# Other widths for the two parts of the last down projection, an earlier norm of the first, and work moved from GpSimd to VectorE

## The chip, the core and the metric

The kernel runs on one core of a Trainium2 chip. Its metric is the device time in microseconds of one launch; lower is better. The kernel computes a whole decoder layer, and the change concerns its last 35 microseconds.

## The reference

One layer of a hybrid decoder for a prompt of 512 tokens and 8 sample sequences of 4 tokens, 544 tokens in all, with 1024 features. Dilated attention, a gated recurrence and a cross attention come first; they are not touched. What matters here is the end, which both groups of tokens share:

```python
def rmsnorm(x, g):
    x32 = x.astype(jnp.float32)
    y = x32 * lax.rsqrt(jnp.mean(x32 * x32, axis=-1, keepdims=True) + EPS)
    return (y * g.astype(jnp.float32)).astype(x.dtype)
...
    x = x + (jax.nn.silu(conv) * (u @ w_up)) @ w_down      # w_down: 2816 x 1024
...
    yp = rmsnorm(yp, norm_final)
    ys = rmsnorm(ys, norm_final)
```

The last norm needs, for each token, the sum of squares over all 1024 features, so over everything that the down projection writes.

## The kernel before

Activations lie transposed: features on the 128 partitions, tokens along the free dimension. The residual `x` is 8 tiles (m = 0 to 7) of 128 features by 544 tokens, called `xr` in the profile. The 2816 hidden features are 22 tiles; the down projections of the first 18 are interleaved with the products that make the hidden tiles. The last four, `h18` to `h21`, come at the end, in the function `last_half(m, c)`: m is the tile of output features, c the part of the tokens. `LAST_CUTS` gives the parts, (first token, count).

Every value of these products is split in a high and a low half of the type fp32r, and three products (high by high, low by high, high by low) make one of nearly full precision. So one call of `last_half` is 4 x 3 = 12 matmuls into one PSUM bank `ps_dz`, each with a weight tile of 128x128 of its own (`wdhz`, `wdlz`). The program first does all 8 tiles of part 0, then all 8 of part 1: 192 matmuls.

Behind each tile, VectorE adds the bank to the residual (`add_to`), ScalarE squares the new residual (`sq_final`, or straight into `acc_final` for m = 0), and `ssq3.add` adds this square to `acc_final`, on GpSimd unless another engine is given. The last tile's squares stay in a tile of their own, `sq_last`. In part 1 the last tile takes another way: ScalarE copies the residual into the bank ahead of the matmuls, which add to it, and the result is read straight from the bank.

`final(c)` is the norm of a part. TensorE multiplies a matrix of ones with `acc_final` and with `sq_last` (plain fp32, each in two passes, `psr_final`), which leaves each token's sum on every partition. ScalarE takes the logarithm (into `r_fin`) and twice the exponential, once into PSUM (`r_final`) and once into SBUF (`r_fin`). Then each of the 8 tiles is scaled into `y` and sent to `yT`. For tiles in `ON_POOL[c]`, ScalarE multiplies by the norm's weights ahead of time in `last_half`, and GpSimd multiplies by `r_fin`; for the others VectorE does both in one operation (SCALAR_TENSOR_TENSOR). The transfers go through SP's queue, but for the odd tiles of part 1, which go through ScalarE's.

The order on the engines is not the order of the text. A recording layer takes all operations with their dependencies and estimated lengths, keeps the order of those marked `tape.main()` on TensorE (the tiles and both norms), and places the others on VectorE, ScalarE, GpSimd and SP by when they are due. Each engine then works its list strictly in order. All recorded operations have line 650 in the profile, transfers line 624, so groups are told apart by the names of their tiles.

The squares are added in the class `SumSq`, whose last line is

```python
                (adder or self.adder).tensor_tensor(self.acc[:, n0:n], self.acc[:, n0:n], sq[:, n0:n], op=ALU.add)
```

Of the kernel before, what the change touches and what calls it, by code (L numbers as in the profile page):

```python
# [22 lines left out]
KT = D // 128  # L23
# [30 lines left out]
LAST_MV = 4  # L54
CUTS = ((0, 256), (256, 288))

LAST_CUTS = ((0, 288), (288, 256))

TILES = (2, 2, 1)
PAIR_LEAD = 10.0  # L60
# [594 lines left out]
def tile_decoder_step(ctx: ExitStack, tc: tile.TileContext, xT, memT, kwT, vw, s0, conv_in, mkT, mv, vecs, cst,  # L655
                      w_first, w_in, w_out, w_cq, w_ck, w_cv, w_co, w_gate, w_up, w_down,
                      yT, kT_out, vT_out, st_out, conv_out, mkT_out, mv_out, ss_out):
    nc = tape = Tape(tc.nc)
# [9 lines left out]
    def A(name, shape=None, dt=F32):  # L668
        return tape.tile(act, shape or [128, FW], dt, tag="a", name=name, bufs=NA)
# [13 lines left out]
    def PF(name):  # L683

        turn[0] += 1
        return PDEC(name) if turn[0] % 3 == 0 else PD(name)
# [18 lines left out]
    def V(name, i=0):  # L705
        return vec[:, VEC_COLS[name][0] + i:VEC_COLS[name][0] + i + 1]
# [129 lines left out]
    def passes(ps, w, xs, n0, n, order, first=True, last=True, loose=False):  # L836
        for at, i in enumerate(order):
            (hi, lo), (xh, xl) = w[i], xs[i]
            for j, (a, b) in enumerate(((hi, xh), (hi, xl), (lo, xh))):
                nc.tensor.matmul(ps[:, :n], a, b[:, n0:n0 + n], start=(first and at == 0 and j == 0),  # L840
                                 stop=(last and at == len(order) - 1 and j == 2), skip_group_check=loose)
# [875 lines left out]
    x = []  # L1717
# [25 lines left out]
    def add_to(m):  # L1743
        def evac(ps, n0, n):
            nc.vector.tensor_tensor(x[m][:, n0:n0 + n], x[m][:, n0:n0 + n], ps[:, :n], op=ALU.add)
        return evac
# [187 lines left out]
    ssq3 = SumSq("final", nc.gpsimd)  # L1934
# [393 lines left out]
    r_fin, last_sq = A("r_fin"), A("sq_last")  # L2328
    hs, k = [hid[j] for j in range(*DOWN_LAST)], DOWN_LAST[1] - DOWN_LAST[0]
    ys, last = {}, []  # L2330
    ON_POOL = (1, 3, 6), (1, 5)

    def y_at(m, c):
        if (m, c) not in ys:
            ys[m, c] = A(f"y{m}_{c}")
        return ys[m, c][:, :LAST_CUTS[c][1]]

    def last_half(m, c):
        n0, n = LAST_CUTS[c]
        cut = slice(n0, n0 + n)  # L2340
        if m == 0 and c == 1:
            tape.gate_at = len(tape.mains) - 1
            nc.sync.dma_start(conv_out, last2)
            nc.scalar.preload_act_table_set(LN_SET)
            tape.gate_at = None
        ps = PF(f"ps_dz{m}_{c}")
        whole = m == KT - 1 and c == 1
        if whole:
            tape.gate_at = len(tape.mains) - 1
            nc.scalar.copy(ps[:, :n], x[m][:, cut])  # L2350
            tape.gate_at = None
        with tape.main():
            passes(ps, held[m], hs, n0, n, range(k), not whole, loose=whole)
        if whole:
            nc.scalar.activation(last_sq[:, cut], ps[:, :n], AF.Square)
            last.append(ps[:, :n])
            return
        add_to(m)(ps, n0, n)
        if m < KT - 1:
            ssq3.add(x[m][:, cut], n0, nc.vector if m >= KT - 2 - c else None)  # L2360
        else:
            nc.scalar.activation(last_sq[:, cut], x[m][:, cut], AF.Square)
        if m in ON_POOL[c]:
            nc.scalar.activation(y_at(m, c), x[m][:, cut], AF.Copy, scale=V("norm_final", m))

    def final(c):
        n0, n = LAST_CUTS[c]
        cut = slice(n0, n0 + n)
        ps = PX(f"psr_final{c}")
        for i, sq in enumerate((ssq3.acc, last_sq)):  # L2370
            nc.tensor.matmul(ps[:, :n], C("ones"), sq[:, cut], start=i == 0, stop=i == 1)
        nc.scalar.activation(r_fin[:, cut], ps[:, :n], AF.Ln, bias=eps, scale=1.0 / D)

        r = PX(f"r_final{c}")[:, :n]
        nc.scalar.activation(r, r_fin[:, cut], AF.Exp, scale=-0.5)
        nc.scalar.activation(r_fin[:, cut], r_fin[:, cut], AF.Exp, scale=-0.5)
        for m in range(KT):
            out = y_at(m, c)
            if m in ON_POOL[c]:
                nc.gpsimd.tensor_tensor(out, out, r_fin[:, cut], op=ALU.mult)  # L2380
            else:
                src, rows = (last[0], r_fin[:, cut]) if c and m == KT - 1 else (x[m][:, cut], r)
                nc.vector.scalar_tensor_tensor(out, src, V("norm_final", m), rows, op0=ALU.mult, op1=ALU.mult)
            (nc.scalar if c and m % 2 else nc.sync).dma_start(yT[128 * m:128 * m + 128, cut], out)

    held = []
    for m in range(KT):
        t, hi, lo = (A(f"{n}z{m}", [128, k, 128], dt) for n, dt in (("wd", F32), ("wdh", F32R), ("wdl", F32R)))
        with tape.early(12.0):
            nc.sync.dma_start(t, w_down[m][:, 128 * DOWN_LAST[0]:128 * DOWN_LAST[1]]  # L2390
                              .rearrange("p (k c) -> p k c", c=128))
            nc.scalar.copy(hi, t)
            nc.vector.tensor_tensor(lo, t, hi.bitcast(F32), op=ALU.subtract)
        held.append([(hi[:, i, :], lo[:, i, :]) for i in range(k)])
        last_half(m, 0)
    for m in range(KT):
        last_half(m, 1)
        if m == 2:
            with tape.main():
                final(0)  # L2400
    with tape.main():
# [76 lines left out]
```

## Time and profile before

| what | value |
|---|---|
| time, median of 3 runs | 813.92 us (813.55 to 814.2) |
| span of the profiled execution, first to last instruction | 813.0 us |
| busy of that span: PE, DVE, ACT, POOL | 802.4, 648.5, 445.0, 102.8 us |
| mean granted TensorE clock | 0.998 |
| part 0 of the last projection (first matmul to first of part 1) | 779.55 to 792.33 us |
| part 1 with the first norm between tiles 2 and 3, to the last matmul's end | 792.33 to 804.60 us |
| start of the second norm on TensorE | 804.77 us |
| first and last scaling of part 1 on VectorE | 806.89, 809.39 us |

The profile gives the span as the time of the profiled execution; the runs are timed outside it. PE is TensorE's matmuls, PEld its weight loads, which overlap them; DVE is VectorE, ACT ScalarE, POOL GpSimd, SP the engine whose queue issues most transfers. A timeline row holds the start, the duration, the engine, the line, the operation, out<-in, the shape, and how many rows were merged (x2); in brackets stand the engine's idle time before it and what ended it. Matmuls overlap, so the distance between two starts is a matmul's cost and the duration is not. A TensorE instruction listed once in the program can be two in the trace, where plain fp32 takes two passes.

### The profile page before, as it was taken

The page shows a single profiled execution, that of the slowest core. Times are in us where ns is not written, and L with a number is a line of the kernel's source. Part 1 is how long each engine was busy: PE and PEld are TensorE (multiplying, and loading weights), DVE is VectorE, ACT ScalarE, POOL GpSimd, SP SyncE. Part 2 cuts the span into 40 slices and gives each one's busy share as a digit, 9 for nine tenths or more (in the row PEclk, how much of TensorE's full clock was granted, in tenths as well). Part 3 has the DMA queues.
Part 4 walks back from the last instruction along what each step waited for, and adds up shares of the span by engine and source line. Part 5 has one row for each costly group of instructions (what it writes and reads, how often), then busy time and mean ns, then how long its engine had stood idle before and what let it go on. Part 6 is the DMA issues. An engine that isn't in the chain of part 4 may idle for free.

```text
span 813.0 us, 18994 instructions
## 1 busy us (share of the span) xinstructions
PE 802.4 (99%) x7531; PEld 755.4 (93%) x7531; DVE 648.5 (80%) x1458; ACT 445.0 (55%) x889; POOL 102.8 (13%) x186
## 2 busy tenths in 40 slices
PE   9999999999999999999999999999999999999996
PEld 9999986787889889999899999999999999999996
DVE  6996689966887897574689999997888788788854
ACT  7643365666657647454567655554554454445433
POOL 0021100010010000002201211211022012210013
PEclk9999999999999999999999999999999999999999
DMA  9449995955942454261734665655565555564503
GB/s 330 151 129 310 308 381 188 320 195 187 288 124 99 162 160 156 59 218 48 229 106 99 157 161 136 162 132 143 130 150 140 133 150 155 130 177 97 153 1 110
DMA packets 93065, 135.47 MB, mean 167 GB/s; under 512 B 6321, under 2 KB 60337, under 8 KB 92977
## 3 DMA queue, kind: packets, MB, share of 16 engines
q1 hardware_dynamic: 86208, 122.79, 46.8%
q0 software_dynamic: 5760, 10.49, 8.3%
q8 instruction: 59, 0.97, 0.5%
q10 hardware_dynamic: 1008, 0.99, 0.4%
q14 instruction: 30, 0.24, 0.1%
HBM read 126.17 MB, written 8.07 MB: 165 GB/s over the span
## 4 chain that ended last, share of the span: by engine, by line
PE 90%; DVE 5%; DMA 2%; ACT 2%; issue 1%; SPq 0%; DVEq 0%
PE ps_d L650 13%; PE ps_ag L650 7%; PE ps_au L650 7%; PE ps_wo L650 6%; PE ps_cu L650 4%; PE ps_cg L650 4%; PE ps_cq L650 3%; PE ps_dz L650 3%; PE ps_co L650 2%; PE ps_z_v L650 2%; PE ps_z_i L650 2%; PE ps_dg L650 2%; PE ps_du L650 2%; PE ps_z_Q L650 2%; PE ps_z_f L650 2%; PE ps_g L650 1%
## 5 line engine op out<-in xcount | busy, mean ns | idle before, releaser
L650 ACT CAST wh<-wr 128x1024 fp32r<-128x1024 f32 (+1 forms) x54 | 46.1, 873 | 45.3 <-PE ps_z_i L650 8.9
L650 DVE TENSOR_TENSOR wl<-wr,wh 128x1024 fp32r<-128x1024 f32 (+1 forms) x54 | 54.3, 1016 | 3.7 <-ACT wh L650 3.6
L650 DVE TENSOR_TENSOR xr<-xr,ps_d 128x256 f32<-128x256 f32 x80 | 34.6, 433 | 11.1 <-PE ps_d L650 10.2
L650 POOL COPY last<-ug 128x16 f32<-128x16 f32 (+1 forms) x44 | 22.6, 534 | 120.2 <-DVE ug L650 119.6
L650 DVE SCALAR_TENSOR_TENSOR cv<-ug,vec,cv 128x560 f32<-128x560 f32 x44 | 35.1, 798 | 2.5 <-ACT cv L650 1.9
L650 ACT ACTIVATE cv<-ug,vec 128x560 f32<-128x560 f32 x22 | 18.8, 856 | 15.5 <-DVE ug L650 15.4
L650 POOL TENSOR_TENSOR hvm<-hsm,cs 64x512 f32<-64x512 f32 x4 | 4.5, 1119 | 161.6 <-ACT hsm L650 161.6
L650 DVE TENSOR_TENSOR cv<-cv,r_ux 128x512 f32<-128x512 f32 (+1 forms) x44 | 18.7, 435 | 3.9 <-ACT cv L650 3.3
L650 ACT ACTIVATE P<-P,mx 128x128 f32<-128x128 f32 (+3 forms) x32 | 17.6, 553 | 6.7 <-DVE mx L650 6.7
L650 ACT ACTIVATE cv<-cv 128x560 f32<-128x560 f32 x22 | 14.8, 674 | 9.1 <-DVE cv L650 9.1
L624 POOL DMA_DIRECT2D S1u<-in_w_up x10 | 8.6, 863 | 87.4 <-DMA S1u<-in_w_up 27.6
L650 ACT COPY keptu<-ps_au 128x272 f32<-128x272 f32 x20 | 7.7, 386 | 21.1 <-PE ps_au L650 21.1
L650 ACT COPY keptg<-ps_ag 128x272 f32<-128x272 f32 x20 | 7.7, 385 | 21.0 <-PE ps_ag L650 20.7
L650 POOL TENSOR_SCALAR cp<-cp,cden 128x256 f32<-128x256 f32 x8 | 8.1, 1019 | 85.7 <-issue 76.2
L650 PE MATMUL ps_co<-coh,wh 128*128 128x256 f32 (+1 forms) x64 | 18.6, 291 | 0.0
L650 PE MATMUL ps_co<-coh,wl 128*128 128x256 f32 (+1 forms) x64 | 18.4, 288 | 0.0
L650 PE MATMUL ps_co<-col,wh 128*128 128x256 f32 (+1 forms) x64 | 18.4, 288 | 0.0
L650 DVE TENSOR_TENSOR xr<-xr,ps_wo 128x256 f32<-128x256 f32 (+1 forms) x16 | 6.8, 435 | 12.6 <-PE ps_wo L650 12.6
L650 DVE TENSOR_TENSOR xr<-xr,ps_dz 128x288 f32<-128x288 f32 (+1 forms) x15 | 6.6, 438 | 12.3 <-PE ps_dz L650 12.3
L650 PE MATMUL psdo<-st,dpt 128*32 128x256 f32 x224 | 16.2, 386 | 0.1
L650 ACT ACT_TABLE_LOAD x11 | 14.1, 1283 | 2.3 <-issue 2.1
L650 PE MATMUL psd<-st,qbd_win 128*32 128x224 f32 x256 | 15.4, 358 | 0.0
(3889 smaller groups left out, 3670.7 us busy)
## 6 DMA issues: line engine op xcount, KB each, us to landing
st<-in_kwT SPq DMA_DIRECT2D x32, 448.0 KB, 5.9
st<-in_vw SPq DMA_DIRECT2D x28, 512.0 KB, 5.7
wd<-in_w_down SPq DMA_DIRECT2D x32, 256.0 KB, 3.1
wr<-in_w_in SPq DMA_DIRECT2D x15, 512.0 KB, 6.6
wrg<-in_w_gate SPq DMA_DIRECT2D x10, 512.0 KB, 4.1
wru<-in_w_up SPq DMA_DIRECT2D x10, 512.0 KB, 4.5
st<-in_mkT SPq DMA_DIRECT2D x8, 512.0 KB, 6.8
wr<-in_w_out SPq DMA_DIRECT2D x8, 512.0 KB, 3.7
```

What stands on the lines that cost most here:

```text
L624: return tape.put(engine, lambda: call(*args, **kw), outs, ins, 0.1, 0.3, size)
L650: return tape.put(engine, lambda: call(*args, **kw), outs, ins, length, lag, size, port, words)
```

## The change

The first part of the last projection gets 352 tokens for 288, the second 192 for 256. The norm of the first part is asked for behind tile 1 of the second part, not behind tile 2. In the first part only tile 1 is scaled by GpSimd, not tiles 1, 3 and 6. In the second part all squares are added by VectorE, not only the last two.

```diff
-LAST_CUTS = ((0, 288), (288, 256))
+LAST_CUTS = ((0, 352), (352, 192))
...
-    ON_POOL = (1, 3, 6), (1, 5)
+    ON_POOL = (1,), (1, 5)
...
         if m < KT - 1:
-            ssq3.add(x[m][:, cut], n0, nc.vector if m >= KT - 2 - c else None)
+            ssq3.add(x[m][:, cut], n0, nc.vector if c or m >= KT - 2 else None)
...
     for m in range(KT):
         last_half(m, 1)
-        if m == 2:
+        if m == 1:
             with tape.main():
                 final(0)
```

What this does to the order: on TensorE, around the first norm (in `ps_dz_1_...` the 1 is the part; the number behind it counts tiles of the whole program; `cs` holds the ones). Before, the norm stands behind the third tile of part 1:

```order
L650 MATMUL ps_dz_1_2058<-h21l,wdhz_2024 128x256
L650 MATMUL ps_dz_1_2058<-h21h,wdlz_2025 128x256
L650 MATMUL psr_final_2060<-acc_final,cs 128x288
L650 MATMUL psr_final_2060<-sq_last,cs 128x288
L650 MATMUL ps_dz_1_2067<-h18h,wdhz_2029 128x256
```

Now it stands behind the second:

```order
L650 MATMUL ps_dz_1_2053<-h21l,wdhz_2018 128x192
L650 MATMUL ps_dz_1_2053<-h21h,wdlz_2019 128x192
L650 MATMUL psr_final_2056<-acc_final,cs 128x352
L650 MATMUL psr_final_2056<-sq_last,cs 128x352
L650 MATMUL ps_dz_1_2065<-h18h,wdhz_2024 128x192
L650 MATMUL ps_dz_1_2065<-h18l,wdhz_2024 128x192
```

The norm moved up by the twelve matmuls of one tile, and all its neighbours changed width.

On VectorE, at the end of part 1 (`xr_918`, `xr_919`, `xr_920` are the residual tiles 5, 6 and 7; `sq_final_5` the squares of tile 5; `y_0` and `y_1` outputs of part 0 and 1). Before:

```order
L650 TENSOR_TENSOR xr_917<-xr_917,ps_dz_1_2069 128x256
L650 SCALAR_TENSOR_TENSOR y_0_2066<-xr_920,vec,r_final_2061 128x288
L650 TENSOR_TENSOR xr_918<-xr_918,ps_dz_1_2071 128x256
L650 TENSOR_TENSOR xr_919<-xr_919,ps_dz_1_2074 128x256
L650 TENSOR_TENSOR acc_final<-acc_final,sq_final_5_2072 128x256
L650 TENSOR_TENSOR acc_final<-acc_final,sq_final_6_2075 128x256
L650 SCALAR_TENSOR_TENSOR y_1_2079<-xr_913,vec,r_final_2078 128x256
```

Now:

```order
L650 TENSOR_TENSOR xr_918<-xr_918,ps_dz_1_2071 128x192
L650 TENSOR_TENSOR acc_final<-acc_final,sq_final_4_2070 128x192
L650 SCALAR_TENSOR_TENSOR y_0_2062<-xr_918,vec,r_final_2057 128x352
L650 TENSOR_TENSOR xr_919<-xr_919,ps_dz_1_2074 128x192
L650 TENSOR_TENSOR acc_final<-acc_final,sq_final_5_2072 128x192
L650 SCALAR_TENSOR_TENSOR y_0_2063<-xr_919,vec,r_final_2057 128x352
L650 TENSOR_TENSOR acc_final<-acc_final,sq_final_6_2075 128x192
L650 SCALAR_TENSOR_TENSOR y_0_2064<-xr_920,vec,r_final_2057 128x352
L650 SCALAR_TENSOR_TENSOR y_1_2079<-xr_913,vec,r_final_2078 128x192
```

Between residual additions there now stand an addition of squares and a scaling of part 0, and one such scaling stands in front of the last addition of squares.

## The prediction

> **What bounds the kernel now.** I read the page first, then the chain of waits for the last 35 us, then the timeline of each engine from 779 us on.
>
> ```profile
> PE 802.4 (99%) x7531; PEld 755.4 (93%) x7531; DVE 648.5 (80%) x1458; ACT 445.0 (55%) x889; POOL 102.8 (13%) x186
> ```
>
> ```profile
> 779.71 17.02 PE ps_dz L650 x132
> 796.74 0.97 PE psr_final L650 x4
> 797.71 7.05 PE ps_dz L650 x60
> ...
> 804.77 1.18 PE psr_final L650 x4
> ...
> 805.97 0.48 ACT r_fin L650
> ...
> 806.47 0.40 ACT r_final L650
> ...
> 806.89 0.93 DVE y L650 x2
> 807.83 0.39 DVEq L2457
> 808.21 1.18 DVE y L650 x3
> ```
>
> TensorE works without a break to 804.6. Then come the norm of the second part (two matmuls over sums of squares), its logarithm and exponential on ScalarE, six row scalings on VectorE to 809.39, and 3.6 us of output transfers and closing. So two things are worth time: the pace of the 192 matmuls `ps_dz`, and the lone tail, which shrinks with the second part's width.
>
> **The change, part by part.** *First part, 352 for 288 columns.* These rows give the paces (starts of instructions):
>
> ```profile
> 779.55 0.29 PE L650 MATMUL ps_dz<-h18h,wdhz 128*128 128x288 f32 x1
> ...
> 792.33 0.28 PE L650 MATMUL ps_dz<-h18h,wdhz 128*128 128x256 f32 x1
> ...
> 796.46 0.28 PE L650 MATMUL ps_dz<-h21h,wdlz 128*128 128x256 f32 x1
> 796.57 0.65 PE L650 MATMUL psr_final<-acc_final,cs 128*128 128x288 f32 x2
> ...
> 797.66 0.28 PE L650 MATMUL ps_dz<-h18l,wdhz 128*128 128x256 f32 x1
> ```
>
> ```profile
> 306.12 0.39 PE L650 MATMUL ps_cv<-wh,mmh 128*128 128x512 f32 x1
> ...
> 308.45 0.40 PE L650 MATMUL ps_cv<-wh,mml 128*128 128x512 f32 x1
> ```
>
> 96 matmuls of 288 columns take 792.33 - 779.55 = 12.78, 0.133 each; 35 steps at 256 take 4.13, 0.118 each; ten steps at 512 take 2.33, 0.233 each. That is a straight line of about 0.45 ns a column, which puts 352 at 0.1616: 96 x 0.0285 = **+2.74**.
>
> *Second part, 192 for 256 columns.* By the same line 192 would take 0.089 and give all of it back. But every one of these matmuls loads its own 128x128 weights, and no row has this dtype between 128 and 256 columns. The nearest:
>
> ```profile
> 305.21 0.19 PEld L650 LDWEIGHTS psr_attS<-sql_attS,blk_r 128*128 128x128 f32 x1
> 305.32 0.19 PEld L650 LDWEIGHTS ps_cv<-wh,mmh 128*128 128x128 f32 x1
> 305.43 0.19 PEld L650 LDWEIGHTS ps_cv<-wh,mml 128*128 128x128 f32 x1
> ```
>
> ```profile
> 411.21 1.88 PEld L650 LDWEIGHTS ps_cos<-cs,com 128*128 128x128 f32 x16
> ```
>
> ```profile
> 411.33 1.85 PE L650 MATMUL ps_cos<-cs,com 128*128 128x16 f32 x16
> ```
>
> ```profile
> L650 PEld LDWEIGHTS psT<-cs,P x80: 137/140/143, 142.6 to 274.2; 128*128 128x128 f32 x80
> ```
>
> ```profile
> 145.06 1.07 PEld L650 LDWEIGHTS psT<-cs,P 128*128 128x128 f32 x10
> ```
>
> `psr_attS` is a matmul of only 128 columns in the same split type, and the loads around it still stand 0.11 apart. The 16 loads of `ps_cos`, whose matmuls have 16 columns, go at (1.88 - 0.19)/15 = 0.113. Transposes go at (1.07 - 0.14)/9 = 0.103, with 0.14 the median length of one. So a full weight load costs about 0.112 however narrow the matmul; at 256 columns it was covered by 0.118 of streaming, at 192 it isn't. I take 0.112, nearest to the same type: 96 x (0.112 - 0.118) = **-0.58**. The bounds are 0.089 (no floor, -2.78) and 0.113 (-0.48).
>
> The Trainium skill (TensorE: Matmul & The Clock Gate, section LDWEIGHTS) has a load take columns/1.2 GHz, 107 ns for 128, whatever the row count, and its section on weight-path modes excludes fp32 from the fast load. By that figure this term would be an estimated -1.06 and the sum 0.5 lower; the trace's 0.110 to 0.113 decides.
>
> *Norm of the first part.* Its four passes ran from 796.57 to the next tile's second matmul at 797.66, less one step of 0.118: 0.97. By width, 352/288, **+0.21**. That it now stands behind tile 1 instead of tile 2 costs TensorE nothing:
>
> ```profile
> 793.10 0.44 ACT L650 ACTIVATE sq_last<-xr 128x288 f32<-128x288 f32 x1 [0.59 <-DVE xr L650]
> ```
>
> its last input, the squares of tile 7, came at 793.54, 1.2 us after the second part began, and now comes at about 1.3, while two tiles take 24 x 0.112 = 2.7. Nor is it a gain in itself, since TensorE does the same work in either place.
>
> TensorE's last `ps_dz` therefore ends 2.74 - 0.58 + 0.21 = 2.37 later, at 806.97 (804.60 before).
>
> *VectorE during the second part.* It gains from GpSimd four additions of squares, which now lie in front of scalings, and two scalings of the first part.
>
> ```profile
> 799.91 0.93 DVE L650 SCALAR_TENSOR_TENSOR y<-xr,vec,r_final 128x288 f32<-128x288 f32 x2
> 801.09 0.51 DVE L650 SCALAR_TENSOR_TENSOR y<-xr,vec,r_final 128x288 f32<-128x288 f32 x1
> ...
> 803.07 0.28 PE L650 MATMUL ps_dz<-h21h,wdlz 128*128 128x256 f32 x1
> 803.38 0.42 DVE L650 TENSOR_TENSOR xr<-xr,ps_dz 128x256 f32<-128x256 f32 x1 [0.98 <-PE ps_dz L650]
> 803.72 0.42 DVE L650 TENSOR_TENSOR acc_final<-acc_final,sq_final 128x256 f32<-128x256 f32 x1
> ...
> 804.29 0.42 DVE L650 TENSOR_TENSOR acc_final<-acc_final,sq_final 128x256 f32<-128x256 f32 x1
> ...
> 806.89 0.48 DVE L650 SCALAR_TENSOR_TENSOR y<-xr,vec,r_final 128x256 f32<-128x256 f32 x1 [2.18 <-ACT r_final L650]
> ...
> 807.74 1.65 DVE L650 SCALAR_TENSOR_TENSOR y<-xr,vec,r_final 128x256 f32<-128x256 f32 x4
> ```
>
> A scaling behind another costs 0.42 at 288 and (1.65 - 0.48)/3 = 0.39 at 256, so about 0.50 at 352 and 0.33 at 192. An addition behind another costs 0.34 at 256, about 0.27 at 192 (0.36 alone). Per tile 0.27 + 0.27 + 0.50 = 1.04 against TensorE's 12 x 0.112 = 1.34, so it keeps up on the whole. The order decides at the end. Tile 6 ends at 805.63; its residual addition starts 0.2 later (803.07 + 0.12 to 803.38 in the rows), 805.83; behind it stand the fifth addition of squares (806.10), a 352-column scaling (806.37) and only then the sixth (806.87), ending 807.23. The second norm needs that one. It starts at 807.30, 0.33 behind TensorE's last tile. Before, the same addition ended at 804.71 and the norm started at 804.77, 0.17 behind. **+0.16**. If the queue runs freely it is zero or slightly less; priced with lone durations it is +0.46 (rivals).
>
> *The tail.*
>
> ```profile
> 797.75 0.50 ACT L650 ACTIVATE r_fin<-psr_final,eps 128x288 f32<-128x288 f32 x1
> 798.28 0.42 ACT L650 ACTIVATE r_final<-r_fin 128x288 f32<-128x288 f32 x1
> ...
> 805.97 0.47 ACT L650 ACTIVATE r_fin<-psr_final,eps 128x256 f32<-128x256 f32 x1 [0.79 <-PE psr_final L650]
> 806.47 0.39 ACT L650 ACTIVATE r_final<-r_fin 128x256 f32<-128x256 f32 x1
> ```
>
> The four norm passes shrink by 64/288 of 0.97, **-0.22**. Logarithm and exponential lose 0.03 for 32 columns, so 0.055 each for 64: **-0.11**. Six scalings lose 0.064 each: **-0.39**. The last transfers carry 96 KB for 128 KB; their row gives no size dependence, and I take **-0.05**, between 0 and a quarter of the 3.6 us behind the last scaling, -0.9; nearer to 0, since the closing has no size.
>
> *What is hidden.* GpSimd's six removed operations
>
> ```profile
> 801.47 0.81 POOL L650 TENSOR_TENSOR y<-y,r_fin 128x288 f32<-128x288 f32 x1
> ...
> 802.24 0.75 POOL L650 TENSOR_TENSOR acc_final<-acc_final,sq_final 128x256 f32<-128x256 f32 x1
> ```
>
> were done before anything waited (the last by 803.0); their place on VectorE is priced above. Two scalings fewer on ScalarE and the later first-part outputs on SP's queue (the last at about 807.8, ahead of the tail's first at 809.4) delay nothing. The few weight splits that change places on VectorE before 779 us stand ahead of tiles that start later than now. Without those covers each would cost at most one operation, 0.5.
>
> **Sum:** 2.74 - 0.58 + 0.21 + 0.16 - 0.22 - 0.11 - 0.39 - 0.05 = +1.76 on the profiled span of 813.0, so 814.8; the median of the three runs, 813.92, lies 0.9 above that span, which gives **815.6** (rounded).
>
> **Rivals.**
> *The width sets the pace.* If the weight load hides at 192 too, the second part runs at 0.089 and TensorE ends at 804.8. VectorE, with 1.04 for TensorE's 1.07, then falls behind through the bunched scalings, and the sixth addition comes at about 805.5: norm +0.8, tail -0.8, 813.9. Did VectorE keep up, 813.2. So not slower than before. For it: the paces at 256, 288 and 512 lie on one line. Against: the 0.11 between loads at 128 columns. Chance 0.09. The Trainium skill (same page, section Back-to-back issue gap) gives 81 ns a load and matmul pair at 128 columns and 131 at 512, an estimated 89 at 192, which is this rival; this trace has 233 ns at 512, so its figures don't fit here.
>
> *A faster load.* At the transposes' 0.103 the second part is another 96 x 0.009 = 0.86 shorter: 814.8; halfway, 815.2. For it: that row; against: `psr_attS` and `ps_cos`. Chance 0.12.
>
> *VectorE late at the end.* If every operation takes its lone duration (0.36, 0.36, 0.58), a tile costs 1.30, nearly TensorE's 1.34, and the bunch of scalings after the first norm isn't caught up: the sixth addition ends at 807.55, the norm starts 0.3 later: 815.9, and up to 816.4 if a scaling more stands in front. For it: the residual addition waits for TensorE in most tiles now, with nothing overlapping. Against: rows one behind the other overlap. Chance 0.13.
>
> **How the numbers follow.** The forecast has 0.66, with its own spread of 815.1 to 816.1 (paces of 352 between 0.160 and 0.1625, loads 0.110 to 0.113). The range of 813.5 to 816.4 takes in the rivals but for the best end of the first. 0.2% is 1.63 us, about what a measurement of this kernel can tell from no change: the forecast lies just beyond it, so slower is 0.58 of its 0.66 share, plus nearly all of the late VectorE: 0.38 + 0.12 = 0.50. Faster is an end of the first rival: 0.05. The rest, 0.45, lies within.
>
> **What would show it.** Right: `ps_dz` matmuls 0.161 apart in the first part and 0.112 in the second, equal to the spacing of their loads; the first part's end near 795.1; the last `ps_dz` near 807.0; the second norm starting behind an addition of squares; from there to VectorE's last scaling about 3.9 (4.6 before). Wrong: a spacing near 0.09 in the second part, or a norm that starts more than 0.5 after the last `ps_dz`.

## The result and the profile after

The changed kernel took 817.21 us (median of 7 runs, 815.73 to 818.59) against 814.2 for the kernel before in the same comparison (7 runs, 813.55 to 815.54): a ratio of 1.0028, 95% interval 1.0017 to 1.0038. It is slower, as forecast, but above the range of 813.5 to 816.4. Two later comparisons gave 1.0019 (1.0010 to 1.0028) and 1.0025 (1.0015 to 1.0035). One of the 35 runs of the kernel before in the first of these two took 2743.4 us, and the ratio leaves it out.

The span of its profiled execution is 815.6 us, 2.6 more than before. The chain of waits at its end:

```profile
780.63 18.10 PE ps_dz L650 x120
798.72 1.21 PE psr_final L650 x4
799.93 6.69 PE ps_dz L650 x60
806.62 0.02 issue
806.64 0.04 DVE xr L650
806.68 0.24 issue
806.91 0.35 DVE acc_final L650
807.27 0.06 DVE y L650
807.33 0.35 issue
807.67 0.36 DVE acc_final L650
808.04 0.04 issue
808.08 0.93 PE psr_final L650 x4
...
809.04 0.43 ACT r_fin L650
...
809.49 0.34 ACT r_final L650
...
809.86 0.81 DVE y L650 x2
```

The chain has a new stretch between TensorE's last tiles and the second norm: residual addition, addition of squares, a scaling of part 0, addition of squares. Before, it went from `ps_dz` straight to the norm. The TensorE rows of the changed kernel give the paces:

```profile
780.46 0.33 PE L650 MATMUL ps_dz<-h18h,wdhz 128*128 128x352 f32 x1
...
795.90 0.25 PE L650 MATMUL ps_dz<-h18h,wdhz 128*128 128x192 f32 x1
...
800.08 0.27 PE L650 MATMUL ps_dz<-h19h,wdhz 128*128 128x192 f32 x1
...
807.67 0.28 PE L650 MATMUL ps_dz<-h21h,wdlz 128*128 128x192 f32 x1
808.08 0.59 PE L650 MATMUL psr_final<-acc_final,cs 128*128 128x192 f32 x2
```

96 matmuls of 352 columns take 15.44, 0.161 each. From 800.08 to 807.67 are 68 steps, 0.112 each. The weight loads of the same kernel stand equally far apart:

```profile
800.10 0.19 PEld L650 LDWEIGHTS ps_dz<-h19l,wdhz 128*128 128x128 f32 x1
800.21 0.19 PEld L650 LDWEIGHTS ps_dz<-h19h,wdlz 128*128 128x128 f32 x1
800.33 0.19 PEld L650 LDWEIGHTS ps_dz<-h20h,wdhz 128*128 128x128 f32 x1
```

So the second part runs at the pace of its weight loads, and the 64 columns moved to the first part are paid there in full. What this stage doesn't explain: the first `ps_dz` starts at 780.46, 0.91 later than the 779.55 before, though nothing on TensorE in front of it was changed. Most of that is already there at the start of the launch. Two rows of the changed kernel and one of the kernel before:

```profile
6.46 0.38 PE L650 MATMUL ps_first<-xm0h,wfh 128*128 128x256 f32 x1 [0.82 <-ACT wfh L650]
...
12.21 0.28 PE L650 MATMUL ps_first<-xm2l,wfh 128*128 128x256 f32 x1
```

```profile
11.40 0.28 PE L650 MATMUL ps_first<-xm2l,wfh 128*128 128x256 f32 x1
```

The same matmul starts 0.81 later. The wait of 0.82 in front, for a split of the first weights, is not in the profile of before.

### The profile page after: what moved, and what is told of

Read it like the earlier page. It is cut to its first block, busy times and chain, and to the rows that moved or that the text cites. A ratio compares the mean times of both kernels' runs of the same rounds, so it can differ in the third digit from the quotient of the medians.

```text
span 815.6 us, 18991 instructions
## 1 busy us (share of the span) xinstructions
PE 804.3 (99%) x7531; PEld 757.8 (93%) x7531; DVE 651.0 (80%) x1464; ACT 444.0 (54%) x887; POOL 100.0 (12%) x180
## 4 chain that ended last, share of the span: by engine, by line
PE 92%; DVE 4%; DMA 1%; issue 1%; ACT 0%; ACTq 0%; DVEq 0%
PE ps_d L650 13%; PE ps_ag L650 7%; PE ps_au L650 7%; PE ps_wo L650 6%; PE ps_cu L650 4%; PE ps_cg L650 4%; PE ps_dz L650 3%; PE ps_cq L650 3%; PE ps_co L650 2%; PE ps_first L650 2%; PE ps_z_v L650 2%; PE ps_z_i L650 2%; PE ps_dg L650 2%; PE ps_du L650 2%; PE psdo L650 2%; PE ps_z_Q L650 2%
## 5 line engine op out<-in xcount | busy, mean ns | idle before, releaser
L650 DVE SCALAR_TENSOR_TENSOR cv<-ug,vec,cv 128x560 f32<-128x560 f32 x44 | 35.1, 798 | 2.5 <-ACT cv L650 1.9
L650 DVE TENSOR_TENSOR xr<-xr,ps_dz 128x352 f32<-128x352 f32 (+1 forms) x15 | 6.7, 444 | 14.0 <-PE ps_dz L650 14.0
```

Source lines behind the costliest of these rows:

```text
L650: return tape.put(engine, lambda: call(*args, **kw), outs, ins, length, lag, size, port, words)
```

## The experiments

The theory (A) is that the wider first part costs in full, that the second gives little back, since a matmul's cost has a floor in its weight load, and that the shorter tail gives back the rest: 1.7 us in all, behind the first `ps_dz`. The other 0.9 is a wandering start. Its rivals are that the change also delays the work in front (B), that VectorE's added work is the cost and not the widths (C), and that 0.112 at 192 columns lies on a flatter line and is no floor (D).

**The changed kernel and the kernel before, again.** The only edit is an empty line, so that line 650 is 651 here.

> The changed kernel once more, on one chip with the kernel before. Theory A (weight loads bound the 192-column matmuls, and everything in front of the last projection only wanders from execution to execution): from the first ps_dz to the end 35.1 us as in its first profile, against 33.45 before, so 1.7 more; the first ps_dz starts anywhere from 779.4 to 780.6; time 1.5 to 2.0 above the kernel before. Rival B (the change also delays the work in front): the first ps_dz starts at 780.3 or later again and the time is 2.4 to 3.2 above.

> The kernel before, unchanged, under another name. A and B: no difference beyond the interval. A: its first ps_dz also moves by up to 1 us against 779.55, since the first transfers of a launch land differently each time. B: it starts at 779.4 to 779.7 again.

> The changed kernel a third time, in a call of its own. Theory A: 35.1 from the first ps_dz to the end again, time 1.6 to 2.0 above the kernel before; the first ps_dz anywhere from 778.5 to 782. If the first comparison's distance of 3.0 between the medians was the change's own: 2.5 or more again.

Each fence shows the first `ps_dz` of one kernel's profiled execution. The changed kernel again:

```profile
779.23 0.33 PE L651 MATMUL ps_dz<-h18h,wdhz 128*128 128x352 f32 x1
```

The kernel before, again:

```profile
780.66 0.29 PE L651 MATMUL ps_dz<-h18h,wdhz 128*128 128x288 f32 x1
```

The changed kernel starts this stage at 780.46, 779.23 and, the third time, 779.50; the kernel before at 779.55 and 780.66. Both repeats of the changed kernel began earlier than the first profile of before, so B falls. The start moved by a little more than A said: 779.23 lies below its 779.4, and 780.66 is 1.11 from 779.55, where up to 1 was expected. From there to the end of the span it is 35.1 in all three profiles of the changed kernel (814.3 - 779.23) and 33.45 in both of the kernel before (814.1 - 780.66): **+1.65**, the same to 0.05. The times: changed 816.21 (11 runs) and 816.71 (12 runs) against 814.62 (35) and 814.9 (17); the kernel before against itself 815.09 (12) against 814.62, 1.0004 (0.9996 to 1.0013). The third distance, 1.8, lies in A's 1.6 to 2.0; the first one's 3.0 was not repeated.

What wanders is seen in two places. One is the waits of TensorE in the first 420 us (waited for: us in all, times, longest). The execution of the experiment `rest_only` below, which began this stage latest of all, at 782.10, has two that the profile of before lacks:

```profile
PE psdo L650 <- DMA st<-in_vw: 0.8, 1, 0.8
PE ps_first L650 <- ACT wfh L650: 0.6, 1, 0.6
```

The first is a load of the cache and the second a split of the first weights. They make 1.4 of its 2.55. The other place is the granted TensorE clock. In two of the eleven profiles, `before_again` and `rest_only`, it fell to 0.5 for 3.4 us at about 133 us; until TensorE is done it is 1.0 everywhere else. In `before_again`, 288-column matmuls stand 0.24 apart during that time, where those of the last projection before the change took 0.133:

```profile
134.13 0.44 PE L651 MATMUL ps_z_v<-xm3h,wh 128*128 128x288 f32 x1
134.37 0.44 PE L651 MATMUL ps_z_v<-xm3l,wh 128*128 128x288 f32 x1
```

From `psS<-cs,z_v` to the next `psin<-cs,hk` these two take 5.25 and 5.22, the other nine 3.7: 1.5 more. Without it, the repeated kernel before would have begun the last projection at an estimated 779.2 (780.66 - 1.5). In `rest_only` the waits' 1.4 and the clock's 1.5 make 2.9, and some 0.3 of that was made up elsewhere. Of the 88 runs of the kernel before in the later comparisons, the 73 with a mean granted clock of 0.997 or more have a median of 814.58, the 15 below it one of 816.06. Why transfers land differently from launch to launch, and why the clock falls in some, wasn't tried.

**Only the widths.**

```diff
 # against the kernel before
-LAST_CUTS = ((0, 288), (288, 256))
+LAST_CUTS = ((0, 352), (352, 192))
```

> Only the widths 352 and 192; norm behind tile 2, GpSimd's work as before. A: ps_dz 0.161 apart in the first part and 0.112 in the second, TensorE's last ps_dz 2.4 later counted from the first; the last addition of squares follows its residual addition without a scaling between, so the second norm starts within 0.1 of the last ps_dz; tail 0.75 shorter; in all +1.5 against before. Rival C (widths cost little, VectorE's extra work made most of the loss): below +0.5.

**All but the widths.**

```diff
 # against the changed kernel
-LAST_CUTS = ((0, 352), (352, 192))
+LAST_CUTS = ((0, 288), (288, 256))
```

> All but the widths: parts of 288 and 256, the first norm behind tile 1, squares and scalings on VectorE. A: no wait is added at these widths, since a tile takes 1.41 and VectorE needs about 1.1: within 0.3 of the kernel before. Rival C: +1 or more.

The widths alone: 1.0020 (1.0011 to 1.0028), 35.06 from the first `ps_dz` to the end. All but the widths: 1.0005 (0.9995 to 1.0014), 33.55. So the widths carry +1.6 and the rest +0.1; C falls. The widths-only kernel shows what the wait for VectorE is worth. Its TensorE and then its VectorE rows:

```profile
807.84 0.28 PE L650 MATMUL ps_dz<-h21h,wdlz 128*128 128x192 f32 x1
808.01 0.59 PE L650 MATMUL psr_final<-acc_final,cs 128*128 128x192 f32 x2
808.54 0.59 PE L650 MATMUL psr_final<-sq_last,cs 128*128 128x192 f32 x2
```

```profile
807.60 0.36 DVE L650 TENSOR_TENSOR acc_final<-acc_final,sq_final 128x192 f32<-128x192 f32 x1 [0.16 <-ACT sq_final L650]
809.99 0.41 DVE L650 SCALAR_TENSOR_TENSOR y<-xr,vec,r_final 128x192 f32<-128x192 f32 x1 [2.03 <-ACT r_final L650]
```

The norm starts 0.17 behind the start of the last `ps_dz`, a little more than the expected 0.1, and not 0.41 as with the whole change. But its second half waits for `sq_last`, the squares of the last tile, so from norm to first scaling it takes 1.98 against 1.78. Of the 0.24 saved, 0.04 reaches the end.

**Narrower still, 416 and 128.**

```diff
 # against the changed kernel
-LAST_CUTS = ((0, 352), (352, 192))
+LAST_CUTS = ((0, 416), (416, 128))
```

> The change with parts of 416 and 128. Theory A (a full weight load takes 0.112, however narrow the matmul): ps_dz 0.190 apart in the first part and still 0.112 in the second; from the first ps_dz to the end about 38.0 us, against 35.10 at 352/192 and 33.45 before, so 4 to 5 us slower than the kernel before. Rival D (the cost goes with the width on a flatter line below 256, and 192 just fell on 0.112): 0.085 or less in the second part, to the end 35.5 or less.

Measured: 821.22 against 814.6, 1.0071 (1.0055 to 1.0086). The loads in the second part:

```profile
798.00 0.19 PEld L650 LDWEIGHTS ps_dz<-h18h,wdlz 128*128 128x128 f32 x1
798.11 0.19 PEld L650 LDWEIGHTS ps_dz<-h19h,wdhz 128*128 128x128 f32 x1
798.23 0.19 PEld L650 LDWEIGHTS ps_dz<-h19l,wdhz 128*128 128x128 f32 x1
```

The pace stays at 0.112 with 128 columns, so D falls: it is a floor. The first part takes 18.15 (0.189 each). To the end it is 38.9, 0.9 more than A said and 5.4 more than before; the medians lie 6.6 apart, where 4 to 5 was expected. Only four runs stand behind the median, and the 1.2 between the two distances stays open. The VectorE rows of the same kernel say why:

```profile
809.02 0.64 DVE L650 SCALAR_TENSOR_TENSOR y<-xr,vec,r_final 128x416 f32<-128x416 f32 x1
809.58 1.08 DVE L650 TENSOR_TENSOR acc_final<-acc_final,sq_final 128x128 f32<-128x128 f32 x3
810.57 2.32 DVE L650 SCALAR_TENSOR_TENSOR y<-xr,vec,r_final 128x416 f32<-128x416 f32 x4
812.80 0.35 DVE L650 SCALAR_TENSOR_TENSOR y<-ps_dz,vec,r_fin 128x128 f32<-128x128 f32 x1
```

The last `ps_dz` starts at 809.84, but three additions of squares stand behind a scaling, and the norm begins at 810.71, 0.87 later. Four scalings of part 0 then fill VectorE up to the tail's. Here its queue does decide.

**At the edge of the floor, 304 and 240.**

```diff
 # against the changed kernel
-LAST_CUTS = ((0, 352), (352, 192))
+LAST_CUTS = ((0, 304), (304, 240))
```

> The change with parts of 304 and 240. A: 240 columns stream in 0.111, as long as a weight load, so 0.112 in the second part and 0.139 in the first; TensorE +0.15, tail -0.2; from the first ps_dz to the end 33.3 to 33.5, as before (33.45). D: a line without a corner puts 240 above 0.114 and the end at 33.7 or more.

Measured: 0.9999 (0.9987 to 1.0011), 33.6 from the first `ps_dz` to the end, 0.1 more than A's bounds and 0.1 less than D's. The steps are 0.140 and 0.112, as A has them. The first rows of the second part, 23 steps in 2.58:

```profile
792.84 0.27 PE L650 MATMUL ps_dz<-h18h,wdhz 128*128 128x240 f32 x1
...
795.42 0.27 PE L650 MATMUL ps_dz<-h21h,wdlz 128*128 128x240 f32 x1
```

At 256 columns it was 0.118, so the corner lies between 240 and 256 columns. The last 0.1 is the norm, which waits for the last addition of squares:

```profile
804.41 0.41 DVE L650 TENSOR_TENSOR acc_final<-acc_final,sq_final 128x240 f32<-128x240 f32 x1 [0.47 <-ACT sq_final L650]
```

No split tried here beat 288 and 256.

**Scalings back to GpSimd, and the norm back behind tile 2.**

```diff
 # pool_y, against the changed kernel
-    ON_POOL = (1,), (1, 5)
+    ON_POOL = (1, 3, 6), (1, 5)
 # tile2, against the changed kernel
-        if m == 1:
+        if m == 2:
```

> The change at 352/192, but tiles 1, 3 and 6 of the first part scaled by GpSimd, as before. Theory A' (the scaling in front of the last addition of squares delays the second norm by 0.12): the last addition now stands right behind the fifth, the norm starts within 0.3 of the last ps_dz's start, as before the change, and the end comes 34.95 after the first ps_dz (35.10 with the change). If the wait isn't that scaling's: 35.10 again.

> The change at 352/192, but the first norm behind tile 2, as before. A: the place of the norm buys and costs nothing, 35.0 to 35.2 from the first ps_dz to the end. Rival E (the earlier norm keeps VectorE's scalings out of the tail, so it was worth something): 35.5 or more, with scalings of the first part in front of the tail's first.

The norm behind tile 2: 1.0022 (1.0011 to 1.0032), 35.1 to the end. Its place is worth nothing, as A has it.

The scalings on GpSimd: 1.0021 (1.0011 to 1.0031), 35.3 to the end, so 0.2 worse where 0.15 better was expected. VectorE's and then GpSimd's rows of this kernel:

```profile
801.14 0.35 DVE L650 TENSOR_TENSOR xr<-xr,ps_dz 128x192 f32<-128x192 f32 x1
801.41 0.80 DVE L650 TENSOR_TENSOR acc_final<-acc_final,sq_final 128x192 f32<-128x192 f32 x1
...
805.16 0.35 DVE L650 TENSOR_TENSOR xr<-xr,ps_dz 128x192 f32<-128x192 f32 x1 [0.72 <-PE ps_dz L650]
805.43 0.57 DVE L650 SCALAR_TENSOR_TENSOR y<-xr,vec,r_final 128x352 f32<-128x352 f32 x1
805.92 0.81 DVE L650 TENSOR_TENSOR acc_final<-acc_final,sq_final 128x192 f32<-128x192 f32 x2
```

```profile
800.15 2.86 POOL L650 TENSOR_TENSOR y<-y,r_fin 128x352 f32<-128x352 f32 x3 [7.27 <-ACT r_fin L650]
```

The planner moved a scaling in front of the fifth addition of squares, so both last additions now come behind it, and the norm starts 0.60 behind the start of the last `ps_dz` instead of 0.41:

```profile
806.19 0.28 PE L650 MATMUL ps_dz<-h21h,wdlz 128*128 128x192 f32 x1
806.79 0.59 PE L650 MATMUL psr_final<-acc_final,cs 128*128 128x192 f32 x2 [0.33 <-DVE acc_final L650]
```

So a scaling in front of the squares does cost, but this edit moved it and didn't take it away; the expectation looked only at the sixth addition.

## Why the prediction was right and where it was wrong

The working held; the level did not. Two lines of the table need the last `ps_dz` of the kernel before; its second norm starts at 804.77:

```profile
804.48 0.28 PE L650 MATMUL ps_dz<-h21h,wdlz 128*128 128x256 f32 x1
```

By the prediction's own steps, against the rows:

| step | predicted | measured |
|---|---|---|
| first part, 352 columns | +2.74 | 15.44 - 12.78 = +2.66 |
| second part and first norm (from its first to its last `ps_dz`) | -0.58 + 0.21 | 11.77 - 12.15 = -0.38 |
| wait for the last addition of squares | +0.16 | 0.41 - 0.29 = +0.12 |
| second norm to first scaling | -0.22 - 0.11 | 1.78 - 2.12 = -0.34 |
| six scalings, first start to last end | -0.39 | 2.11 - 2.50 = -0.39 |
| transfers and closing | -0.05 | about 0 |
| sum | +1.76 | +1.65 to +1.7 |

The choice on which the sum rests was 0.112 for a full weight load, taken from `psr_attS` and `ps_cos`. By the Trainium skill's 107 ns (TensorE: Matmul & The Clock Gate, section LDWEIGHTS) the second part would have been an estimated 0.5 shorter; the trace has 0.112, at 192 and at 128 columns alike. The rival with 0.089 is excluded. With it goes, for this type, the Trainium skill's 81 to 131 ns a pair (same page, section Back-to-back issue gap): here it is 112 at 128 columns and 233 at 512. The faster load of the transposes isn't that of these matmuls. The rival of a late VectorE is bounded: the norm's wait cost about 0.04 at the end, since `sq_last` is the next gate, and only at 416 and 128 does VectorE hold up the tail.

The step that failed is the last one of the sum, which sets the level: "the median of the three runs, 813.92, lies 0.9 above that span". It took the median of three runs as the kernel's level. The later medians of the same kernel were 814.2, 814.62, 814.6, 814.9 and 815.09, so 0.3 to 1.2 higher. The profile says the same in another way. In every execution here that has both, the time lies 1.8 above the span, to within 0.1: 817.37 and 815.6, 816.11 and 814.3, 815.92 and 814.1, and 814.82 and 813.0 for the parts of 304 and 240. So the profiled execution of before, with 813.0, took about 814.8, if the same holds for it, and the sum against its own time gives 814.8 + 1.76 = 816.6, in place of 815.6. (813.92 + 1.76 is 815.68, which the prediction put down as 815.6.) With 814.6 for the level, the measured +1.65 gives 816.25. The changed kernel's medians are 817.21, then 816.21 and 816.71. The first comparison's distance of 3.0 was followed by 1.6 and 1.8, so what lifts 817.21 above the other two is put down to the spread of launches; no trace here singles it out.

The range failed with it. It was made of the bounds of the costs alone and left out that the work in front wanders: the first `ps_dz` started between 778.58 and 782.10 in the eleven profiles, and the 17 runs of the kernel before in the last comparison lie between 813.65 and 817.17. Medians of a few runs moved by 1.2 for the kernel before (813.92 to 815.09) and 1.0 for the changed one. With 1 us more on the upper side, from those spreads, the range would have held. The chance of slower was put at one half, since the forecast lay just beyond 0.2%, 1.63 us; of the three ratios two lie above 1.002 and one below.

What stays open: the three ratios center on 1.0024, about 1.95 us, and the traces give 1.65. The intervals hold both.

## What to carry to other kernels

Where every matmul of this type loads new 128x128 weights, narrowing it below the point at which streaming takes as long as the load (here 0.112 us, between 240 and 256 columns) gives nothing back, so a split for a shorter tail should stop there. Price such a floor from rows with the narrowest matmuls in the trace, even if their widths are far from the one in question. When a time is forecast from a profile, add the gain to the profiled execution's own time or to the median of many runs, and let the range hold the spread of launches as well as the bounds of the costs. Compare two profiles from a common matmul on, and look at the granted clock ahead of it, before a later start is put down to a change.

## What the runs showed of the hardware that was not expected

VectorE was held up beside GpSimd. An addition of squares, both inputs in SBUF, took 0.80 at 801.41 while GpSimd multiplied tiles from 800.15 to 803.01, in the rows above of the kernel with three scalings on GpSimd. The residual addition in front of it, with one input in PSUM, kept its 0.35 under the same GpSimd work. In the changed kernel, where GpSimd had ended its one multiplication (801.63 to 802.57), the same addition took 0.35:

```profile
802.90 0.35 DVE L650 TENSOR_TENSOR acc_final<-acc_final,sq_final 128x192 f32<-128x192 f32 x1
```

GpSimd itself shows no such loss: its three took 2.86, 0.95 each, against 0.94 for the one in the changed kernel.

The Trainium skill (SBUF — State Buffer, section Who interferes with whom) says that a VectorE instruction with two SBUF inputs contends with a GpSimd instruction that reads SBUF; these rows agree.

The other surprise is told above: in two of the eleven profiles the granted clock fell to 0.5 for 3.4 us in the middle of the launch, and TensorE's work there took 1.5 us longer.
